# Decoder layer on one core: key rows in two other buffers, seven casts put ahead of copies, early scores half a tile sooner

## The chip, the cores and the metric

The kernel runs on one core of a Trainium2 chip. A core has five engines that run beside each other, each with its own queue of instructions: TensorE (PE, matrix products and transposes through the array; its weight loads are listed apart as PEld), VectorE (DVE), ScalarE (ACT), GpSimd (POOL) and SyncE (SP, which here only issues transfers between the main memory and the core). They wait for one another through semaphores. An engine takes its instructions in the order of its queue, so one that waits holds up all behind it.

The metric is the time of one execution on the device in microseconds (us). The profile is of one execution; its span runs from the first to the last instruction.

## The reference, cut to what matters

One layer of a decoder, for a prompt of 2048 tokens (D_MODEL 1024) and for 8 sequences of 4 sample tokens with 8192 earlier tokens each in a paged cache. All is in float32.

```python
h = rms_norm(x, pre_g)
z = h @ w_in                     # 11 parts of 512 columns
ca, cb, cg, pu, pg, q, k, v, sg, mq, mg = split(z)
mk, mv = split(rms_norm(mem, g) @ w_mem_kv)     # 256 memory tokens
y_c, conv_new = conv_branch(ca, cb, ...)        # depthwise conv of 31 taps, LayerNorm, pointwise
y_p, pool_new = pool_branch(pu, ...)
y_s = sb_fn(q, k, v, sb_bias)                   # stick-breaking attention, 8 heads x 64
y_m = mem_attend(mq, mk, mv)                    # softmax attention, 4 heads x 128
mix = concat([y_c * silu(cg), y_p * silu(pg), y_s * silu(sg), y_m * silu(mg)])
out = rms_norm(mix @ w_out, post_g)
return x + out, conv_new, pool_new, k, v        # then a last rms_norm; k, v, mk, mv are outputs too
```

## The kernel before

**Stages.** First the projection `z = h @ w_in`, which lasts for some 1490 us and has the cache attention of the sample tokens, the convolution and the memory attention woven into it; then the stick-breaking attention of the prompt; then the product with `w_out`. The prompt goes through the projection in two parts of 1024 tokens; part 0 carries the 32 sample tokens too.

**The projection.** `z_groups` (L786) goes over groups of weight columns (128 columns of one kind: q, k, v, ca and so on), and in each over tiles of tokens: three in part 0 (384, 384, 288), two of 512 in part 1. One tile is a product of 24 matmuls (`mm3`, L236): eight slices of the depth, three products each, because a float32 value is split into a high and a low part of a faster type. The generator yields after half of the 24 and after the tile; at every yield the main loop makes one step of all running tasks, and a task puts its own matmuls between two half tiles of the projection. "Half a tile" in the title is one such step.

**Weights.** `load_w` (L222) loads 128 columns (512 KB) through SP into one of two buffers `wr`; `split_w` (L229) casts them on ACT to the high part `whi` (L232) and subtracts on POOL or DVE for the low part `wlo` (L233); both have two buffers. A cast can run once the load is there and the product that used its buffer has ended; the next load can go once the subtract is done. `fill_w` keeps two weights split and two loaded.

**Memory tokens.** Between the tiles of q2, q3 and k0 in part 0, `mem_tokens` (L404) makes eight products of the memory (`mz`, 256 columns) with weights of its own, in one order with the others. `mem_rows` evacuates them (L424) and splits them for the attention (L418, L419).

**Evacuation.** `z_evac` (L674) takes a finished tile from PSUM. For q and k, ACT copies it to `zt` (L683), DVE casts the high part `hl` (L685), POOL subtracts the low part (L686), and SP stores both (L688). For k and v the task `natural` (L364) transposes `zt` on PE (L370), ACT copies the rows to `nat` (L372), and SP stores them to the output (L375).

**Buffers.** `small` is a tag of four buffers of 128 x 512, shared by `zt`, `nat` of k, gate tiles and others. `mkT` and `mvn` are one buffer each of the same size; the memory attention loads keys and values of one head into them (`mem_kv`, L667). A new tile of a tag waits until an old one has been used for the last time; for a tile that is stored, until the store has landed.

**Histories.** `params_and_histories` loads rows of old states (`ht`, L462) and transposes them on PE (`hps`, L478) between tiles of q2.

**Early scores.** When the sample's cache attention has ended, `sb_early` (L1260) loads keys and queries of the first two blocks of the prompt's attention (L1236, L1237), waits some steps, and makes the first two score tiles `Se` (L1253) between the last half tiles of the projection; ACT turns them into gates (L1257, L1258). DVE and POOL then form the weights.

**Order.** Only PE runs in the order in which the program was written (`manual_schedule`). The queues of ACT, DVE, POOL and SP are put in order by a planner, which runs the program on a model clock and takes what is ready. `tc.issue_after(ins)` adds an edge: what the block issues on the engine of `ins` stands behind `ins` in that engine's queue. It is an order, not a wait.

Of the kernel before, what the change touches and what calls it, by code (L numbers as in the profile page):

```python
# [8 lines left out]
F32 = mybir.dt.float32  # L9
# [9 lines left out]
P = 128  # L19
D = 1024  # L20
# [16 lines left out]
SMALL = 4  # L37
# [50 lines left out]
def kernel(  # L88
# [9 lines left out]
    pe, act, dve, pool, sp = nc.tensor, nc.scalar, nc.vector, nc.gpsimd, nc.sync  # L98
# [52 lines left out]
    def tp_tile(name):  # L151
        return tps.tile([P, 512], F32, tag="tp", name=name)

    def z_tile(name):
        return zps.tile([P, 512], F32, tag="z", name=name)
# [12 lines left out]
    table = [act.activation(out=first, in_=eps_t, func=AF.Sqrt)]  # L168
# [53 lines left out]
    def load_w(it):  # L222
# [3 lines left out]
        wq.dma_start(raw_, src[:, o : o + P].rearrange("(d p) n -> p d n", p=P))  # L226
        return raw_

    def split_w(raw, nm):  # L229
        lo = wp.tile([P, ND, P], F32R, tag="wlo", name=f"wlo{nm}", bufs=2)  # L230
        hi = wp.tile([P, ND, P], F32R, tag="whi", name=f"whi{nm}", bufs=2)
        act.copy(hi, raw)  # L232
        (dve if nm in SECOND else pool).tensor_tensor(out=lo, in0=raw, in1=hi.bitcast(F32), op=ALU.subtract)  # L233
        return hi, lo

# [13 lines left out]
    st = zx.enter_context(tc.tile_pool(name="st", bufs=2, side="left"))  # L249
# [5 lines left out]
    def small(name):  # L255
        return st.tile([P, 512], F32, tag="small", name=name, bufs=SMALL)

    def k4(name, shape, dt):
        return st.tile(shape, dt, tag="k4", name=name, bufs=K4)
# [104 lines left out]
    def natural(zt, N, np_, tok, c, out_ap, scratch, srow, nm):  # L364

        yield
        nb = np_ // P
        pt = tp_tile(f"nt{nm}")
        for j in range(nb):
            pe.transpose(pt[:, P * j : P * (j + 1)], zt[:, P * j : P * (j + 1)], ident)  # L370
        nat = small(f"nat{nm}") if scratch is None else k4(f"nat{nm}", [P, D], F32)
        act.copy(nat[:, : np_], pt[:, : np_])  # L372
        nv = nat[:, : np_].rearrange("p (j n) -> p j n", n=P)
        dst = out_ap[tok : tok + np_, P * c : P * (c + 1)].rearrange("(j p) n -> p j n", p=P)
        wq.dma_start(dst, nv)  # L375
        if scratch is not None:
            wq.dma_start(scratch[tok : tok + np_, P * c : P * (c + 1)].rearrange("(j p) n -> p j n", p=P), nv)
        if N > np_:
            pt2 = tp_tile(f"ns{nm}")
            pe.transpose(pt2[:NS, :P], zt[:, np_:N], ident)  # L380
            nat2 = small(f"nas{nm}")
            act.copy(nat2[:NS, :P], pt2[:NS, :P])
            for dst in srow:
                wq.dma_start(dst[:, P * c : P * (c + 1)], nat2[:NS, :P])
# [19 lines left out]
    def mem_tokens(mp, M):  # L404

        for c in range(8):
            ps = z_tile(f"mz{c}")
            for _ in mm3(ps, *wsplit[0, "mem", c], M["hi"], M["lo"], 0, NMEM):
                pass
            del wsplit[0, "mem", c]  # L410
            fill_w()
            tasks.add(mem_rows(mp, ps, c))
            yield
# [230 lines left out]
        for r0, r1, dst in rows:  # L644
            wq.dma_start(dst, o[r0:r1])

    state = {"att": 0, "early": 0}

    def z_open(part, kind, c):

# [23 lines left out]
    def z_evac(part, kind, c, ti, c0, c1, ps, s):  # L674
        a0 = PART * part
        N = c1 - c0
        np_ = min(c1, PART) - c0
        nm = f"{part}{kind}{c}_{ti}"
        tok = a0 + c0
        if kind in ("q", "k"):  # L680
            zt = small(f"zt{nm}")
            with tc.issue_after(table[6].ins) if nm == "0q0_0" else ExitStack():
                act.activation(out=zt[:, :N], in_=ps[:, :N], func=AF.Copy, scale=0.125 if kind == "q" else 1.0)  # L683
            hl = k4(f"hl{nm}", [P, 2, 512], F32R)
            dve.tensor_copy(hl[:, 0, :np_], zt[:, :np_])  # L685
            pool.tensor_tensor(out=hl[:, 1, :np_], in0=zt[:, :np_], in1=hl[:, 0, :np_].bitcast(F32),  # L686
                               op=ALU.subtract)
            wq.dma_start((qd if kind == "q" else kd)[c, :, :, tok : tok + np_], hl[:, :, :np_].bitcast(F32))  # L688
            if N > np_:
                pool.tensor_copy((qsT if kind == "q" else ksT)[:, c, :], zt[:, np_:N])  # L690
            if kind == "k":
                tasks.add(natural(zt, N, np_, tok, c, kp, None, (kso,), nm))
        elif kind == "v":
            zt = small(f"zt{nm}")
            act.copy(zt[:, :N], ps[:, :N])
            tasks.add(natural(zt, N, np_, tok, c, vp, vd, (vso, vsd), nm))
        elif kind in ("cg", "sg", "pg", "mg"):
            sg = small(f"sg{nm}")
            act.activation(out=sg[:, :N], in_=ps[:, :N], func=AF.Sigmoid)
            if kind == "pg":  # L700
                dve.tensor_tensor(out=sg[:, :N], in0=ps[:, :N], in1=sg[:, :N], op=ALU.mult)
                tasks.add(pool_out(c, state["d"], part, c0, c1, ti, sg, s["plw"]))
            elif kind == "mg":
                gt = state["g"][:, c0:c1]
                dve.tensor_tensor(out=gt, in0=ps[:, :N], in1=sg[:, :N], op=ALU.mult)
                if N > np_:
                    pool.tensor_copy(gms[:, c, :], gt[:, np_:N])
            else:
                dve.tensor_tensor(out=sg[:, :N], in0=ps[:, :N], in1=sg[:, :N], op=ALU.mult)
                gdst = gcd if kind == "cg" else gsd  # L710
                wq.dma_start(gdst[c, :, tok : tok + np_], sg[:, :np_])
                if N > np_:
                    if kind == "cg":
                        wq.dma_start(gcd[c, :, SEQ : SEQ + NS], sg[:, np_:N])
                    else:
                        pool.tensor_copy(gss[:, c, :], sg[:, np_:N])
        elif kind == "ca":
            U = s["U"]
            act.copy(U[:, CH + c0 : CH + c0 + np_], ps[:, :np_])
            if N > np_:  # L720
                act.copy(us_s[:, c, :, CH:], ps[:, np_:N].rearrange("p (b t) -> p b t", t=TS))
        elif kind == "cb":
            U = state["U"]
            sg = small(f"sg{nm}")
            act.activation(out=sg[:, :N], in_=ps[:, :N], func=AF.Sigmoid)
            uu = U[:, CH + c0 : CH + c0 + np_]
            pool.tensor_tensor(out=uu, in0=uu, in1=sg[:, :np_], op=ALU.mult)
            if N > np_:
                uv = us_s[:, c, :, CH:]
                pool.tensor_tensor(out=uv, in0=uv, in1=sg[:, np_:N].rearrange("p (b t) -> p b t", t=TS),  # L730
                                   op=ALU.mult)
        elif kind == "pu":
            pf = s["pf"]
            act.copy(pf[:, PH + c0 : PH + c0 + np_], ps[:, :np_])
            if N > np_:
                act.copy(ps_s[:, c, :, PH:], ps[:, np_:N].rearrange("p (b t) -> p b t", t=TS))
        elif kind == "mq":
            hl = k4(f"mh{nm}", [P, 2, 512], F32R)

            act.activation(out=hl[:, 0, :N], in_=ps[:, :N], func=AF.Copy, scale=-(P ** -0.5))  # L740
            dve.scalar_tensor_tensor(out=hl[:, 1, :N], in0=ps[:, :N], scalar=-(P ** -0.5), in1=hl[:, 0, :N].bitcast(F32),
                                     op0=ALU.mult, op1=ALU.subtract)
            if N > np_:
                dve.tensor_copy(mqs[:, c, :], ps[:, np_:N])
            state["att"] += 1
            tasks.add(mem_attend(c, part, c0, np_, hl, state["g"], s["kv"]))
# [22 lines left out]
    raw, wsplit = {}, {}  # L769
# [490 lines left out]
    def sb_early(load, blk, sbr, bps, early):  # L1260

        room = sbr.tile([P, 16, P], F32, tag="V", name="early", bufs=2).rearrange("p (n j b) c -> p n j (b c)", n=4, j=2)
        for n in range(2):
            blk[0, n] = load(0, n)
        for _ in range(4):
            yield
        for hh in range(2):
            S = bps.tile([P, 512], F32, tag="AT", name=f"Se{hh}", bufs=2).rearrange("p (j k) -> p j k", j=2)
            Q, KT, _ = blk[0, 0]
            sb_scores(S, hh, 0, 2 * P, Q[hh], KT[0, hh, 0])  # L1270
            early[hh] = room[:, 2 * hh], room[:, 2 * hh + 1]
            sb_gates(S, hh, 2 * P, *early[hh])
            yield
# [541 lines left out]
    with tc.tile_pool(name="mem", bufs=2, side="right") as mp:  # L1815
# [23 lines left out]
        mem = mem_tokens(mp, M)  # L1839
# [29 lines left out]
    due, blk, early = 0.0, {}, {}  # L1869
# [269 lines left out]
```

## Time and profile before

| | |
|---|---|
| median of 3 runs | 2387.06 us (2386.06 to 2393.02) |
| the profiled execution | 2387.03 us |
| its span | 2385.3 us |
| mean granted clock of TensorE | 0.987 |
| waits of PE on ACT, POOL or a transfer, at places that the change touches | the rows mz, hps, nt0k, nt1k, z1k and S of the table of waits |
| mean load of the transfer engines | 234 GB/s |

How to read it. A row of a timeline is: start (us from the span's start), length, engine, line of the kernel, operation, what is written and what is read, shape, how many were merged (x3), and in brackets how long the engine had been idle and what it waited for. Tiles of one kind share a name: `zt0k` is a tile of keys of part 0, `nt1k` the transposes of keys in part 1, `whi0mem` the high part of a memory weight. A row of the table of waits is: total us, times, longest. A row of the table by stretches gives busy time and number of instructions of PE, PEld, DVE, ACT and POOL, then the clock that TensorE was granted (1.00 is full), the share of the transfer engines, and GB/s.

### The profile page before, as it was taken

To read this page: it belongs to the slowest core of one execution; us is meant where nothing else is said; L and a number is where in the kernel's file an instruction comes from. 1 tells how busy PE (TensorE), PEld (TensorE's weight loads), DVE (VectorE), ACT (ScalarE), POOL (GpSimd) and SP (SyncE) were. 2 spreads that over 40 slices of the span, in tenths; PEclk is the share of its full clock that TensorE was granted. 3 is DMA by queue.
4 is the path that set the end of the run, shared out by engine and by line. 5 is a ranking of instruction groups with operands and counts; after the bars stand their busy time and mean duration, and the time that the engine had idled before them with its cause. 6 is when DMAs were issued, how large, how long until landed. Compare 5 with 4: busy or idle time off the path is not lost. (4 is left out here: it accounts for less than half of the span.)

```text
span 2385.3 us, 42238 instructions
## 1 busy us (share of the span) xinstructions
PE 2283.3 (96%) x16024; PEld 1774.9 (74%) x16024; DVE 1717.9 (72%) x2428; ACT 1120.3 (47%) x1947; POOL 1282.7 (54%) x1322
## 2 busy tenths in 40 slices
PE   7999999999999999999999999799999999989996
PEld 7898888888888677777777777455555557878875
DVE  5342796969657564577787868878888966777897
ACT  5322243242442222234242424788899875444554
POOL 3454545555565555545546462699877763531231
PEclk9999999999999999999999999899999999999999
DMA  6678977878778899987877875667443206866774
GB/s 212 196 257 290 349 270 259 286 249 291 246 262 316 296 327 331 327 283 260 305 263 262 269 268 150 165 201 215 123 107 79 78 19 218 289 196 207 238 236 162
DMA packets 336869, 557.94 MB, mean 234 GB/s; under 512 B 27986, under 2 KB 212434, under 8 KB 320267
## 3 DMA queue, kind: packets, MB, share of 16 engines
q1 hardware_dynamic: 281290, 286.53, 38.7%
q0 software_dynamic: 55376, 268.72, 31.8%
q8 instruction: 126, 2.06, 0.3%
q14 instruction: 77, 0.62, 0.1%
HBM read 465.09 MB, written 90.68 MB: 233 GB/s over the span
## 5 line engine op out<-in xcount | busy, mean ns | idle before, releaser
L957 DVE STREAM_TRANSPOSE T<-kt 128x1024 f32<-128x1024 f32 x256 | 308.7, 1226 | 190.0 <-PE sSA L970 179.0
L924 POOL DMA_INDIRECT vt<-in_cache_v_dram,idv x256 | 252.8, 987 | 261.6 <-PE sO L1009 200.6
L610 DVE SCALAR_TENSOR_TENSOR cacc<-U,par,cacc 128x512 f32<-128x512 f32 x480 | 359.9, 750 | 11.0
L1335 POOL TENSOR_TENSOR be<-be,E 128x512 f32<-128x512 f32 (+3 forms) x316 | 300.7, 963 | 70.0 <-DVE E L1326 22.5
L1326 DVE TENSOR_TENSOR_SCAN E<-gam,cr,ZM 128x513 f32<-128x513 f32 x192 | 233.3, 1264 | 23.3 <-ACT gam L1257 13.9
L924 POOL DMA_INDIRECT kt<-in_cache_k_dram,idk x128 | 128.5, 1004 | 195.0 <-DVE T L957 152.1
L1346 PEld LDWEIGHTS AT<-ident,be 128*128 128x128 f32 x1082 | 118.1, 143 | 137.0 <-ACT at L1352 40.9
L1959 PE MATMUL acc<-wohi,mh 128*128 128x512 f32 (+1 forms) x480 | 193.3, 403 | 1.5 <-ACT mh L1704 0.8
L1257 ACT ACTIVATE gam<-S,nbias_bc 128x1024 f32<-128x1024 f32 (+1 forms) x158 | 170.2, 1077 | 47.3 <-ACT be L1258 15.4
L1959 PE MATMUL acc<-wolo,mh 128*128 128x512 f32 (+1 forms) x480 | 189.0, 394 | 0.0
L1346 PE MATMUL AT<-ident,be 128*128 128x128 f32 x1082 | 161.4, 286 | 20.9 <-DVE at L1350 9.1
L1253 PE MATMUL S<-kT,Q 128*128 128x512 f32 (+1 forms) x632 | 176.5, 403 | 4.8 <-ACT be L1258 4.8
L1959 PE MATMUL acc<-wohi,ml 128*128 128x512 f32 x448 | 176.9, 395 | 4.1 <-DVE ml L1715 4.1
L1258 ACT ACTIVATE be<-S,bias_bc 128x1024 f32<-128x1024 f32 (+1 forms) x158 | 169.1, 1070 | 0.0
L1362 PE MATMUL av<-at,V 128*64 128x512 f32 (+3 forms) x640 | 153.1, 558 | 3.9 <-DVE sbo L1367 3.9
L970 PE MATMUL sSA<-T,W 128*32 128x128 f32 x4096 | 140.5, 277 | 2.3 <-DVE T L957 1.4
L970 PEld LDWEIGHTS sSA<-T,W 128*32 128x32 f32 x4096 | 105.6, 110 | 37.4 <-issue 30.8
L1009 PE MATMUL sO<-vt,saT 128*32 128x512 f32 x1024 | 122.3, 592 | 0.0
L1253 PEld LDWEIGHTS S<-kT,Q 128*128 128x128 f32 x632 | 106.7, 196 | 18.2 <-ACT be L1258 5.4
L1323 DVE TENSOR_TENSOR_SCAN E<-gam,ZM 128x384 f32<-128x384 f32 (+1 forms) x124 | 94.6, 811 | 33.1 <-ACT gam L1257 25.7
L1352 ACT COPY at<-AT 128x512 f32<-128x512 f32 x192 | 108.9, 650 | 20.1 <-PE AT L1346 19.9
L1715 DVE TENSOR_TENSOR ml<-mr,mh 128x512 fp32r<-128x512 f32 x108 | 87.2, 812 | 30.7 <-ACT mh L1704 30.6
(577 smaller groups left out, 6039.9 us busy)
## 6 DMA issues: line engine op xcount, KB each, us to landing
Q<-qd SPq DMA_DIRECT2D x64, 256.0 KB
mr<-mixd SPq DMA_DIRECT2D x32, 512.0 KB
mr<-mixd SPq DMA_DIRECT2D x48, 256.0 KB
xtp<-in_x_prompt_dram SPq DMA_DIRECT2D x16, 512.0 KB
kT<-kd SPq DMA_DIRECT2D x64, 128.0 KB
ws<-in_w_out_dram SPq DMA_DIRECT2D x16, 512.0 KB
wsd<-ws SPq DMA_DIRECT2D x16, 512.0 KB
msd<-mr SPq DMA_DIRECT2D x32, 256.0 KB
```

Source lines behind the costliest of these rows:

```text
L610: dve.scalar_tensor_tensor(out=ps, in0=U[:, a + k : a + k + H], scalar=wd[:, k : k + 1], in1=ps, op0=ALU.mult, op1=ALU.add)
L924: pool.indirect_dma_start(out=dst, out_offset=None, in_=rows, in_offset=bass.IndirectOffsetOnAxis(ap=idx, axis=0))
L957: S["turn"] = dve.transpose(T[:, 2 * hh : 2 * hh + 2].rearrange("p s j t -> p (s j t)"), kt[:, 2 * hh : 2 * hh + 2].rearrange("p s j d -> ...
L970: pe.matmul(sSs[n][32 * g : 32 * g + 32, P * ml : P * (ml + 1)], lhsT=W[:, jj, :], rhs=T[:, :, jj, :], start=i == 0, stop=i == 3, tile_pos ...
L1253: pe.matmul(S[:, j, :w], lhsT=Q[:, x, P * (q2 + j) : P * (q2 + j + 1)], rhs=kt[:, :w], start=x == 0, stop=x == 1)
L1257: act.activation(out=ga, in_=S[:, :, :w], func=AF.Sigmoid, bias=nbias_bc[:, h : h + 1], scale=-1.0)
L1258: act.activation(out=be, in_=S[:, :, :w], func=AF.Sigmoid, bias=bias_bc[:, h : h + 1])
L1326: dve.tensor_tensor_scan(out=E[:, j][:, ::-1], data0=g_[:, j][:, ::-1], data1=ZM[:, 0:1].to_broadcast([P, 513]), initial=carry[hh, q2][:, ...
L1335: pool.tensor_tensor(out=be[:, j, :m], in0=be[:, j, :m], in1=E[:, j, 513 - w : 513 - w + m], op=ALU.mult)
L1346: pe.transpose(ap_[:, P * qt : P * (qt + 1)], A[hp, qb, kc, hh, qt][:, P * r : P * (r + 1)], ident)
L1362: pe.matmul(av[64 * hh : 64 * hh + 64, c], lhsT=V[:, 4 * kc + r, 64 * hh : 64 * hh + 64], rhs=ats.pop((hp, qb, kc, r, hh))[:, c], start=dg ...
L1959: pe.matmul(o[:rows], lhsT=m[a][:, k, :rows], rhs=W[prod, 4 * h + k][w], start=not cont and h == k == n == 0, stop=h == 1 and k == 3 and n ...
```

## The change

Three things. A row tile of keys takes the buffers `mkT`, `mvn` and `small` in turn, by a counter that runs over all 20 of them, where all came from `small`. While the memory products run (from product 0 up to and not including product 7), the copy `zt` of a q or k tile stands behind the newest weight cast in ACT's queue. And `sb_early` waits three steps instead of four before its scores.

```diff
+    casts = []
+
     def split_w(raw, nm):
         lo = wp.tile([P, ND, P], F32R, tag="wlo", name=f"wlo{nm}", bufs=2)
         hi = wp.tile([P, ND, P], F32R, tag="whi", name=f"whi{nm}", bufs=2)
-        act.copy(hi, raw)
+        casts.append(act.copy(hi, raw))
...
         for j in range(nb):
             pe.transpose(pt[:, P * j : P * (j + 1)], zt[:, P * j : P * (j + 1)], ident)
-        nat = small(f"nat{nm}") if scratch is None else k4(f"nat{nm}", [P, D], F32)
+        if scratch is None:
+            tag = ("mkT", "mvn", "small")[state["nat"] % 3]
+            state["nat"] += 1
+            nat = st.tile([P, 512], F32, tag=tag, name=f"nat{nm}", bufs=SMALL if tag == "small" else 1)
+        else:
+            nat = k4(f"nat{nm}", [P, D], F32)
...
         for c in range(8):
+            state["mem"] = c < 7
             ps = z_tile(f"mz{c}")
...
-    state = {"att": 0, "early": 0}
+    state = {"att": 0, "early": 0, "mem": False, "nat": 0}
...
             zt = small(f"zt{nm}")
-            with tc.issue_after(table[6].ins) if nm == "0q0_0" else ExitStack():
+            before = table[6] if nm == "0q0_0" else casts[-1] if state["mem"] else None
+            with tc.issue_after(before.ins) if before is not None else ExitStack():
                 act.activation(out=zt[:, :N], in_=ps[:, :N], func=AF.Copy, scale=0.125 if kind == "q" else 1.0)
...
         for n in range(2):
             blk[0, n] = load(0, n)
-        for _ in range(4):
+        for _ in range(3):
             yield
```

## The prediction

> **What bounds the kernel now.** I read the page first (busy times, slices), then the table of waits for TensorE alone, then the timelines of all engines around each of its waits in the projection. The page:
>
> ```profile
> span 2385.3 us, 42238 instructions
> ...
> PE 2283.3 (96%) x16024; PEld 1774.9 (74%) x16024; DVE 1717.9 (72%) x2428; ACT 1120.3 (47%) x1947; POOL 1282.7 (54%) x1322
> ```
>
> PE works 96% of the span, its order is written by hand, and no other engine is above 74%. So time is won only where PE stands still, 102 us in all, or runs slowly. The table of PE's waits over the whole span (total us, how often, longest) has these rows for what the change touches:
>
> ```profile
> PE S L1253 <- ACT be L1258: 4.8, 2, 3.0
> ...
> PE nt0k L370 <- ACT zt0k L683: 3.5, 2, 2.1
> PE nt1k L370 <- ACT zt1k L683: 2.5, 1, 2.5
> PE z1k L242 <- ACT xhi L218: 2.5, 1, 2.5
> PE mz L242 <- POOL wlo0mem L233: 2.4, 1, 2.4
> ...
> PE hps L478 <- DMA ht<-in_state_conv_dram: 1.3, 1, 1.3
> PE mz L242 <- ACT whi0mem L232: 1.2, 1, 1.2
> ```
>
> A wait also costs what comes after it. In the table by stretches (length; PE, PEld, DVE, ACT, POOL busy; granted clock; DMA) these follow a wait directly; the second one follows the shorter of the two nt0k waits (3.5 less 2.1 is 1.4):
>
> ```profile
> 66.00:70.00 4.00, 3.72 (x19) 3.72 (x19) 0.00 (x0) 0.00 (x0) 0.23 (x1) 0.58 0.55 163
> 122.00:126.00 4.00, 4.00 (x24) 3.99 (x25) 2.19 (x1) 0.52 (x2) 2.97 (x3) 1.00 0.82 251
> 152.00:156.00 4.00, 4.00 (x20) 4.00 (x19) 0.09 (x1) 1.44 (x3) 1.01 (x1) 0.58 1.05 424
> 794.00:798.00 4.00, 4.00 (x11) 2.93 (x11) 3.79 (x6) 0.03 (x1) 0.00 (x0) 0.61 0.30 114
> 832.00:836.00 4.00, 4.00 (x42) 2.96 (x42) 1.36 (x3) 0.59 (x1) 3.62 (x2) 0.67 0.81 298
> ```
>
> After the waits of 2.1 us and more the granted clock falls to about 0.6 for four microseconds, a loss of 4 x 0.42 = 1.7 us (66, 152), 1.6 (794) and 1.3 (832); after the short wait it stays at 1.00.
>
> **Part 1: the cast ahead of the copy.** The edge ties seven copies (q2_1 to k0_1), but in the timeline six of them already stand behind the cast in question. Only q2_1's moves:
>
> ```profile
> 61.95 0.49 ACT L683 ACTIVATE zt0q<-z0q 128x384 f32<-128x384 f32 x1 [4.23 <-PE z0q L242]
> 62.34 1.04 ACT L232 CAST whi0mem<-wr0mem 128x1024 fp32r<-128x1024 f32 x1
> ```
> ```profile
> 58.59 1.00 POOL L686 TENSOR_TENSOR hl0q<-zt0q,hl0q 128x384 fp32r<-128x384 f32 x1 [4.13 <-ACT mhlk L418]
> ...
> 63.89 2.34 POOL L233 TENSOR_TENSOR wlo0mem<-wr0mem,whi0mem 128x1024 fp32r<-128x1024 f32 x1
> ```
> ```profile
> 51.47 0.56 SPq L226 DMA_DIRECT2D wr0mem<-in_w_mem_kv_dram  x1
> ...
> 66.26 0.37 SPq L226 DMA_DIRECT2D wr0q<-in_w_in_dram  x1
> ...
> 67.30 0.44 SPq L462 DMA_DIRECT2D ht<-in_state_conv_dram  x1
> ```
> ```profile
> 53.88 0.28 PE L242 MATMUL mz<-mhi,whi0mem 128*128 128x256 f32 x1
> ...
> 56.59 0.28 PE L242 MATMUL mz<-mhi,wlo0mem 128*128 128x256 f32 x1
> ...
> 61.69 0.57 PE L478 MATMUL hps<-ident,ht 120*128 120x120 f32 x4
> ...
> 71.97 0.60 PE L478 MATMUL hps<-ident,ht 120*128 120x120 f32 x4 [1.31 <-DMA ht<-in_state_conv_dram]
> ```
>
> ACT stood idle 4.23 us in front of the copy, and the weight behind it had been asked for at 51.47, ten microseconds earlier. The cast's buffer is free when memory product 0 ends, 56.59 + 0.28 = 56.87. So it goes there: cast to about 58, POOL's subtract (2.34, with the 1.00 of hl0q before or after it) to 60.3 to 61.9. PE wants it at 61.69 + 0.57 = 62.3: both mz waits go, 3.6 us, and with them the slow stretch. Product 1 then needs what product 0 took (53.88 to 56.87, 3.0 us) and ends at 65.3. Now something else is late: the next transposes need the histories' rows, whose load stands on SP behind wr0q's, and that waits for the same subtract (63.89 + 2.34 = 66.23). With qd's store, which waits for hl0q, also in that queue, I put wr0q's load at 62.0 instead of 66.26, the histories' 1.04 later, their arrival again 71.97 - 67.30 = 4.67 after the issue: 67.7 instead of 71.97. Gain 4.3. Bounds: 3.4, if hl0q and the subtract are queued the worse way round; 6.7, if the planner puts the histories' load first (71.97 to 65.3). The new wait, 67.7 - 65.3 = 2.4 us, may bring a slow stretch of 1.7; I take off half, 0.9. [...]
>
> **Part 2: key rows in idle buffers.** 20 row tiles (12 in part 0, 8 in part 1) leave the four small buffers in two of three cases. Nothing is added: same copies, same stores. What waited for the buffers:
>
> ```profile
> 151.15 0.49 ACT L683 ACTIVATE zt0k<-z0k 128x384 f32<-128x384 f32 x1 [4.72 <-DMA out_dram<-nat0k]
> ...
> 792.47 0.59 ACT L372 COPY nat1k<-nt1k 128x512 f32<-128x512 f32 x1 [2.06 <-DMA out_dram<-nat1k]
> ...
> 831.10 0.60 ACT L683 ACTIVATE zt1k<-z1k 128x512 f32<-128x512 f32 x1 [3.79 <-DMA out_dram<-nat1k]
> ```
>
> All three waits are for a store that still reads a small buffer. With one row tile in three there, the buffer that each copy gets is four allocations old and holds no open store. At 151 PE gains 2.1 + 1.7 = 3.8; at 831, 2.5 + 1.3 = 3.8: in both the copy waited longer (4.72, 3.79) than PE did (2.1, 2.5), so without the store it is there when PE asks. The 1.4 us wait near 121 stays: its copy is behind a cast, not a store. At 792 it is the row copy itself, with the x casts queued behind it on ACT; without its wait they run 2.06 us sooner, but their DVE subtracts do not:
>
> ```profile
> 789.74 2.33 DVE L610 SCALAR_TENSOR_TENSOR cacc<-U,par,cacc 128x512 f32<-128x512 f32 x3
> 793.58 1.29 DVE L219 TENSOR_TENSOR xlo<-xpsp,xhi 128x512 fp32r<-128x512 f32 x2 [1.51 <-ACT xhi L218]
> ```
>
> DVE is free at 792.07, so PE's second product comes 793.58 - 792.07 = 1.5 us sooner, and the 1.6 of the slow stretch goes or not: 1.5 to 3.1, I take 2.2 (with xlo moved as well, the full 2.5 + 1.6 = 4.1). Queues: the two single buffers are reloaded for the memory attention, and these loads now go behind the last key stores on SP instead of early:
>
> ```profile
> L501 PE MATMUL ms<-mkT,mh0mq x96: 276/279/388, 335.8 to 699.6; 128*128 128x256 f32 x96
> ...
> L669 SPq DMA_DIRECT2D mkT<-mkd x8: 319/385/745, 75.7 to 1364.8; - x8
> ```
>
> The first load moves from 75.7 to about 165; its first reader is at 335.8. The old owner is done at 699.6, 80 us before part 1's first row tile. I price the move at nothing; SP's idle time covers it (rival 2 has the case without).
>
> **Part 3: early scores.** Eight matmuls change places with half a tile; PE's sum is the same.
>
> ```profile
> 1490.42 0.59 ACT L616 COPY acc<-cacc 128x512 f32<-128x512 f32 x1 [6.64 <-DVE cacc L610]
> 1490.90 0.70 ACT L1257 ACTIVATE early<-Se,nbias_bc 128x512 f32<-128x512 f32 x1
> ...
> 1493.67 1.15 ACT L1257 ACTIVATE gam<-S,nbias_bc 128x1024 f32<-128x1024 f32 x1
> ```
> ```profile
> 1478.93 0.60 SPq L1237 DMA_DIRECT2D Q<-qd  x1
> ```
> ```profile
> 1487.17 0.64 PE L1253 MATMUL Se<-kT,Q 128*128 128x256 f32 x4
> ```
>
> The scores were there from 1487.8, but ACT stood 6.64 us at the copy of the convolution's sum. The copy, four gates of the scores and one activation more then run to 1493.67. If the planner, seeing the scores sooner, puts the four gates (1490.42 to 1493.67 is 3.25, two of its six run 0.48, so four take 2.3) ahead of that copy, the attention's first gates and PE's S wait (4.8) come 2.3 sooner; if not, nothing. I take 1.1. On the other side: the last load that both scores need is issued at 1478.93, and Se would start at about 1484.4, 5.5 us later, above the 4.67 of part 1; were the loads as late as today's start, PE would lose 2.8.
>
> **Sum:** 4.3 - 0.9 + 3.8 + 3.8 + 2.2 + 1.1 = 14.3 us. The profiled execution took 2387.03 us (span 2385.3 and 1.7 around it), the median of the runs is 2387.06, so both give 2372.7. After 850 us nothing in the PE table is bound to a fixed time (most waits lie in the attention and the output, on ACT, DVE and POOL), so the gain should reach the end.
>
> **Rivals.** (1) Refilled stalls, time within 0.3%: PE finds the next-late thing at each place. Histories' rows as late as now, DVE's subtract at 792 as late as now, no early gates: only 3.8 + 3.8 stay, less 1.7 for one more slow stretch, 5.9: 2381.1. For it: in part 1 of the sum two other things really are late by 2.4 and 1.5. Against: at 151 and 831 I see none.
> (2) SP held by the moved loads: a load of mkT or mvn behind a key store waits for that store to land. Place: SP from 850. Price: in the crowded stretch a row store issued at 784.52 freed its buffer at 792.47, 8 us, so the weight load due at 853.81 would go some 5 us late:
>
> ```profile
> 784.52 0.66 SPq L375 DMA_DIRECT2D out_dram<-nat1k  x1
> ...
> 853.81 0.38 SPq L226 DMA_DIRECT2D wr1v<-in_w_in_dram  x1
> ```
> ```profile
> 876.27 1.05 ACT L232 CAST whi1v<-wr1v 128x1024 fp32r<-128x1024 f32 x1 [3.21 <-PE z1v L242]
> ```
>
> Its cast is 22 us after the issue (876.27), so it decides only when the hold passes about 16 us; then each further us is lost, and the gain of 14 is gone at a hold of 30: about 2387. [...]
> (3) Slower: the planner orders ACT, DVE, POOL and SP by a clock of its own, and both new rules shift that clock for everything behind them. Place: the sample's 64 blocks, PE scores, ACT gates, DVE scan, PE transposes, where PE hardly waits now. A gate put behind a row copy (0.59) in each block would cost up to 64 x 0.59 = 38 us; it decides from 14.3 / 64 = 0.22 us a block; at 0.4 the time is 2387 - 14.3 + 25.6 = 2398. For it: PE's order is fixed and can't give way. Against: the edges touch 57 to some 110 us and the buffers two short stretches.
>
> **Chances.** Forecast 0.78, refilled 0.11, SP held 0.04 (half of it slower), planner's order 0.07. 0.3% of 2387 is 7.2 us, about what a measurement here can tell from no change. Faster 0.78, same 0.13, slower 0.09. Range: the best of all terms is 6.7 + 3.8 + 3.8 + 4.1 + 2.3 = 20.7, 2366, with 1 us spare; upwards it takes in rival 1 and a little loss to the new order, 2383.
>
> **What the profile after would show.** Right: whi0mem near 57 to 58 and ahead of zt0q, the two mz rows gone from PE's waits, hps waiting 2 to 3 us instead; no wait of ACT for nat0k or nat1k stores, rows nt1k gone and nt0k down to 1.4; z1k waiting for xlo, about 1.5; the granted clock 1.00 around 152 and 832; gates of Se ahead of acc. The forecast fails if PE's table has new rows in the sample's blocks, or a weight row for v in part 1.

## The result and the profile after

The changed kernel takes 2381.61 us (median of 18 runs, 2373.86 to 2392.21), the kernel before, measured beside it, 2388.41 us (18 runs, 2383.04 to 2396.03). The ratio is 0.9972, with a 95% interval of 0.9962 to 0.9982: 6.8 us faster, between 4.3 and 9.1. The forecast was 14.3 us, 2372.7. The sign was right; less than half of the gain came.

The profiled execution of the changed kernel took 2378.62 us. The head of its page:

```profile
span 2376.9 us, 42227 instructions
...
PE 2279.8 (96%) x16024; PEld 1772.0 (75%) x16024; DVE 1720.7 (72%) x2428; ACT 1119.1 (47%) x1947; POOL 1277.5 (54%) x1322
```

TensorE (PE) now idles 2376.9 - 2279.8 = 97.1 us, where it was 102.0. Its table of waits (total us, how often, longest) has, for what the change touches:

```profile
PE S L1262 <- ACT be L1267: 4.8, 2, 3.0
PE hps L486 <- DMA ht<-in_state_conv_dram: 2.7, 1, 2.7
...
PE nt0k L372 <- ACT zt0k L692: 1.3, 1, 1.3
...
PE smt L1175 <- DMA mkb<-in_cache_mem_k_dram: 1.0, 1, 1.0
PE nt0v L372 <- ACT zt0v L704: 1.0, 1, 1.0
...
PE z1k L244 <- ACT xhi L218: 0.3, 1, 0.3
```

The rows of mz and nt1k are gone, nt0k is down to the 1.3 behind a cast, z1k to 0.3, and the histories' wait has grown to 2.7. At each place aimed at, the profile shows what was meant. S is as before. Two rows are new, nt0v and smt, 1.0 each.

Stretches of the changed kernel at those places (PE, PEld, DVE, ACT, POOL busy; granted clock; DMA share; GB/s):

```profile
66.00:70.00 4.00, 1.99 (x16) 2.00 (x16) 2.80 (x6) 0.97 (x3) 2.35 (x1) 1.00 0.79 287
138.00:142.00 4.00, 4.00 (x20) 4.00 (x20) 2.06 (x14) 0.00 (x0) 3.33 (x4) 0.61 1.08 364
150.00:154.00 4.00, 4.00 (x26) 3.96 (x25) 2.22 (x1) 1.14 (x5) 3.28 (x3) 1.00 0.67 229
786.00:790.00 4.00, 3.48 (x18) 2.54 (x17) 3.77 (x7) 1.54 (x4) 0.00 (x0) 1.00 1.01 331
828.00:832.00 4.00, 4.00 (x57) 2.27 (x55) 1.57 (x2) 1.43 (x3) 0.43 (x1) 1.00 1.12 362
```

The clock is full where it had dropped to about 0.6. But it drops at a place where it had not, 138 to 142 us, although PE is busy for all of the four microseconds around it.

Laid side by side by their matmuls, the two traces are 13 us apart at 2037 us and 8.4 at the end: the changed kernel seems to lose 4.5 us in the output stage. The queues' orders are the same in both from 1545 us on. That made the first question: does the output stage hand the gain back, do new waits eat it, or is one of the two profiles an odd draw?

### The profile page after: what moved, and what is told of

It reads as the page before. It is cut to its first block, busy times and chain, and to the rows that moved or that the text cites. A ratio compares the mean times of both kernels' runs of the same rounds, so it can differ in the third digit from the quotient of the medians.

```text
span 2376.9 us, 42227 instructions
## 1 busy us (share of the span) xinstructions
PE 2279.8 (96%) x16024; PEld 1772.0 (75%) x16024; DVE 1720.7 (72%) x2428; ACT 1119.1 (47%) x1947; POOL 1277.5 (54%) x1322
```

## The experiments

**How a profile is taken apart.** The span is cut at the same matmuls in every kernel. In each stretch I take PE's idle time, and half of the busy time that lies at half clock. These two are what the change can move; what is left of the span is 2260 to 2264 us in all kernels. Theory A: the stalls were real and their removal reaches the end, but the forecast priced them from one execution, and they differ from one to the next. Theory B: the output stage hands gain back. Theory C: the new waits nt0v and smt, and the drop at 138 us, belong to the change. Theory D: part 3 costs something, by moving gates and loads to a worse place.

**One part at a time.** First the cast alone:

```diff
-        act.copy(hi, raw)
+        casts.append(act.copy(hi, raw))
...
+            state["mem"] = c < 7
...
-            with tc.issue_after(table[6].ins) if nm == "0q0_0" else ExitStack():
+            before = table[6] if nm == "0q0_0" else casts[-1] if state["mem"] else None
+            with tc.issue_after(before.ins) if before is not None else ExitStack():
```

> Kernel: the kernel before with part 1 alone (the cast of a memory weight ahead of the product tiles' copies). Theory A (the idle time that the change removes is real and reaches the end; the slow-clock stretches behind the stalls were counted as certain, but occur in only about half of the executions): the two mz waits (3.6 us) are gone, the histories' wait grows from 1.3 to about 2.7, so 2.2 us less idle time and about half of a 1.7 us stretch: about 3 us faster in the median (1.5 to 4), and the end of TensorE's work is as much earlier as the stretch behind 70 us, give or take slow stretches that come and go in the output stage in either direction. Theory B (the output stage hands back 4 to 5 us whenever the work ahead of it comes sooner): 3 to 4 us earlier at 1550 us, no earlier at the end, ratio 1.000. Theory C (part 1 itself costs something later, the slow stretch at 138 us being its doing): earlier by 4 at 70 us, by 2.7 from 142 us on, and a slow stretch right behind the histories' 32-column products in this profile too.

Then the key rows alone:

```diff
-        nat = small(f"nat{nm}") if scratch is None else k4(f"nat{nm}", [P, D], F32)
+        if scratch is None:
+            tag = ("mkT", "mvn", "small")[state["nat"] % 3]
+            state["nat"] += 1
+            nat = st.tile([P, 512], F32, tag=tag, name=f"nat{nm}", bufs=SMALL if tag == "small" else 1)
+        else:
+            nat = k4(f"nat{nm}", [P, D], F32)
```

> Kernel: the kernel before with part 2 alone (key rows in turn in the two idle buffers and the small ones). Theory A: idle time removed at 147, 789 and 821 us is 2.2 + 2.0 + 2.5 = 6.7 us, new waits nt0v and smt (1.0 each) take 2.0 of it, and of the three slow stretches of 1.6 about half count in the median: 4.7 + 2.4, so about 6 to 7 us faster (4.5 to 8). Theory B: about 9 us earlier at 1550 us, 4 to 5 of it lost again in the output stage, 4 to 5 us faster, with the loss at the same rows as in the changed kernel (2050 to 2080 and 2240 us). Theory C (the new waits nt0v behind 210 us and smt behind 960 us belong to part 2): both rows are in this profile at about 1.0 each, and not in that of part 1 alone.

The early scores alone:

```diff
-        for _ in range(4):
+        for _ in range(3):
             yield
         for hh in range(2):
```

> Kernel: the kernel before with part 3 alone (the early scores half a tile sooner). Theory A: nothing ahead of 1470 us changes; the wait S stays at 4.8 us, since the copy of the convolution's sum stays ahead of the gates; gain 0 to 1.5 us, not to be told from none. Theory B: as A, and the output stage stays as it was, since its work starts at most 1.5 us sooner. Theory D (the planner moves loads and gates at this place to the bad): slower by 1 to 3 us, with a longer wait of the first scores or of the first scan.

And the changed kernel with that last edit undone, so parts 1 and 2 together:

> Kernel: the changed kernel with the early scores back in their old place (parts 1 and 2 without part 3). Theory A: within 1.5 us of the changed kernel, so 5 to 8 us faster than before. Theory B: the same total, and the output stage loses 4 to 5 us against the kernel before, as it does in the changed kernel. Theory D (part 3 is what loses): 9 us or more faster than before, the output stage as before or the first scan sooner.

Measured beside 35 runs of the kernel before (median 2389.93), with 12 runs each:

```
                       median us   ratio    95% interval
part 1 alone           2385.93     0.9985   0.9975 to 0.9994
part 2 alone           2384.72     0.9984   0.9972 to 0.9996
part 3 alone           2393.18     1.0013   1.0000 to 1.0025
parts 1 and 2          2383.51     0.9978   0.9964 to 0.9991
```

Part 1 is worth 3.6 us (1.4 to 6.0), as forecast (3.4). Part 2 is worth 3.8 (1.0 to 6.7), not 9.8, and less than the 6 to 7 expected of it alone. Part 3 gains nothing that can be told: alone its interval begins at no change and lies on the slower side (3.1 us slower, 0 to 6.0, where Theory A expected a gain of 0 to 1.5), and without it the changed kernel has 0.9978, with it 0.9972, each inside the other's interval. Theory D is neither shown nor excluded by this: the longer wait of the first scores that it expected isn't there, S is 4.8 in part 3 alone as before (a small wait of ACT that part 3 brings is told further below). From 1960 us to the end, idle time and the loss to half clock together are:

```
kernel before, first profile   40.4
changed kernel                 44.8
part 1 alone                   44.9
part 2 alone                   43.1
part 3 alone                   44.9
parts 1 and 2                  44.0
```

Part 3 alone changes nothing ahead of 1470 us and brings the output stage no earlier (its trace is 3.5 us behind there), and it has the same 44.9. So Theory B falls: the odd one is the profile of the kernel before. Theory C falls as well for nt0v: the row of 1.0 stands in all four, part 3 alone among them, and below in the unchanged kernel. The row smt stands in none of the four, nor in any other profile shown below.

**The stalls differ between executions.** Part 1 alone leaves the small buffers as they were. Its table of waits has no row for nt1k (2.5 us in the first profile), but more of the other two:

```profile
PE nt0k L372 <- ACT zt0k L687: 5.8, 3, 2.4
...
PE z1k L244 <- ACT xhi L218: 2.9, 1, 2.9
```

So the unchanged kernel was profiled again, three times, and the changed one twice.

> The kernel before, unchanged, a second profiled execution. Theory A (the first profile of the kernel before was a lucky draw in the stretches that no edit touches, and the four kernels with parts of the change show the usual values): from 1960 us to the end the idle time and the loss to slow-clock stretches are together 43 to 45 us, not the 40.4 of the first profile, and from 200 to 760 us TensorE idles 5.5 to 7 us, not 4.3; the span is 2386 to 2391. The stalls that the change aims at vary too: idle and slow loss 7 to 8 us from 40 to 100 us, 4 to 7 from 100 to 200, 3.5 to 9 from 760 to 860. Theory B (the output stage loses 4 to 5 us because of the change): 40 to 41 us again from 1960 us on.

> The changed kernel, unchanged, a second profiled execution. Theory A: idle and slow loss 3.5 to 5 us from 40 to 100 us and 1.0 from 760 to 860 us as before, since those stalls are gone for good; from 100 to 200 us anything from 3.5 to 9, since the wait for a key store at 150 us comes back in some executions; 43 to 45 from 1960 us on; median 6 to 8 us below the kernel before. Theory B: the same span, and from 100 to 200 us the 3.9 of the first profile again.

> The kernel before, unchanged, a third profiled execution, for how often the stalls that part 2 removes occur at all. Theory A (their size is set by when a store lands, and that differs from one execution to the next): the sum of ACT's waits for key rows' stores that reach TensorE (nt0k beyond its 1.3, nt1k, z1k beyond 0.3) lies anywhere from 2 to 7 us; the first profile had 6.8, the second 2.2. From 1960 us on idle and slow loss are 43 to 46 us. Rival (the second profile was the odd one): 6 to 7 us again, and idle and slow loss of 8 to 9 us from 760 to 860 us.

> The kernel before, unchanged, a fourth profiled execution: as for the one before it. Theory A: idle and slow loss from 760 to 860 us anywhere from 2 to 9 us, mean over the executions without part 2 about 6, not the 8.7 that the prediction was made from.

> The changed kernel, unchanged, a third profiled execution. Theory A: 1.0 us of idle time from 760 to 860 us and 3.5 to 3.8 from 40 to 100 us, as in both profiles so far; from 100 to 200 us 2.0 to 2.2, unless the wait for a row store at 150 us comes back (once in five executions with part 2 so far).

In the second profile of the kernel before, PE's waits have these rows:

```profile
PE nt0k L370 <- ACT zt0k L683: 2.3, 2, 1.3
PE z1k L242 <- ACT xhi L218: 1.5, 1, 1.5
...
PE nt0v L370 <- ACT zt0v L695: 1.0, 1, 1.0
```

and in the third:

```profile
PE nt0k L370 <- ACT zt0k L683: 3.9, 2, 2.6
PE z1k L242 <- ACT xhi L218: 2.9, 1, 2.9
...
PE nt0v L370 <- ACT zt0v L695: 1.0, 1, 1.0
...
PE nt1k L370 <- ACT zt1k L683: 0.9, 1, 0.9
```

The same program waits 0, 0.9 or 2.5 us for nt1k. For the first and the second profile of the kernel before, the stretch from 760 to 860 us reads so (columns as above):

```profile
760.00:860.00 100.00, 94.52 (x743) 72.88 (x741) 57.79 (x74) 29.59 (x54) 52.33 (x49) 0.97 0.89 303
```
```profile
760.00:860.00 100.00, 97.82 (x811) 75.70 (x810) 62.72 (x80) 32.93 (x60) 56.84 (x51) 1.00 0.94 327
```

PE stands still for 5.5 us in the one and 2.2 in the other, and the clock is 0.97 in the one and full in the other. All kernels without the edits of the next paragraphs, idle time plus loss to half clock, cut at the same matmuls:

```
                       40-100  100-200  760-860  1460-1540  1960-end
before, 1st profile    7.4     6.0      8.7      15.8       40.4
before, 2nd            7.5     3.1      2.2      14.0       46.5
before, 3rd            7.8     6.4      7.4      14.1       45.1
before, 4th            7.4     5.7      6.4      13.4       43.2
part 3 alone           7.6     4.3      9.2      13.9       44.9
part 1 alone           3.6     6.8      3.6      14.1       44.9
part 2 alone           7.7     3.8      1.0      13.4       43.1
parts 1 and 2          5.0     8.8      1.0      13.8       44.0
changed, 1st           3.6     3.9      1.0      13.7       44.8
changed, 2nd           5.5     2.0      1.0      14.0       45.5
changed, 3rd           5.5     2.2      1.0      13.3       45.8
```

From 760 to 860 us the five executions with part 2 all have 1.0; the six without it run from 2.2 to 9.2. That stall is gone for good, but it was not always there. The means with and without the part in question differ by 2.9 us (40 to 100, part 1), 1.2 (100 to 200, part 2), 5.3 (760 to 860, part 2) and 0.4 (1460 to 1540, part 3): 9.8 in all. The second comparison of the changed kernel gave 2383.14 us (7 runs) against 2389.65, ratio 0.9967 (0.9953 to 0.9980), 7.9 us. The spread was wider than expected: the second profile of the kernel before has 3.1 and 2.2 us where 4 to 7 and 3.5 to 9 stood, and 46.5 where 43 to 45 stood. The second of the changed kernel misses its ranges too, with 5.5 where 3.5 to 5 stood, 2.0 where 3.5 to 9 stood and 45.5 where 43 to 45 stood. The third and the fourth of the kernel before lie inside what Theory A expected, and so does the third of the changed kernel; but in the third of the kernel before the waits for stores make 6.1 us, which its rival, 6 to 7, allowed as well.

**The wait that came back.** With parts 1 and 2, one execution lost 8.8 us between 100 and 200 us. Its ACT and its SP queue:

```profile
154.92 0.41 ACT L692 ACTIVATE zt0k<-z0k 128x288 f32<-128x288 f32 x1 [5.21 <-DMA out_dram<-nat0k]
```
```profile
140.00 0.56 SPq L382 DMA_DIRECT2D out_dram<-nat0k  x1
```

The same two in the first profile of the changed kernel:

```profile
149.99 0.40 ACT L692 ACTIVATE zt0k<-z0k 128x288 f32<-128x288 f32 x1
```
```profile
137.91 0.56 SPq L382 DMA_DIRECT2D out_dram<-nat0k  x1
```

In part 0 a group has three tiles, and the rotation puts the third one's row tile, with the sample rows (nas) behind it, in small buffers. In a ring of four, the next group's third product tile then gets the buffer of that row tile, whose store was issued 12 to 15 us before. In one execution it had landed by 149.99, in the other not until 154.9. Theory: give the sample rows the free columns of the row tile, so that every small buffer returns to its own user after a whole group.

```diff
-            nat2 = small(f"nas{nm}")
+            nat2 = small(f"nas{nm}") if scratch is not None else nat[:, 384:512]
```

> The changed kernel, with the sample tokens' key rows (32 x 128) written into free columns of the row tile that was just filled instead of a small buffer of their own, so that in part 0 each of the four small buffers comes back to its own user after a whole group of three tiles, and no product tile follows a stored row tile of the group before. Theory A (the wait at 150 us came back because a product tile takes the small buffer of a row store issued some 10 to 15 us earlier, in a stretch where the transfers are full): idle from 100 to 200 us 2.1 to 2.3 (the wait of 1.3 behind the weight's cast alone), no wait of the product tiles' copies for a store there, and 1.5 to 3 us faster in the median than the changed kernel. Rival (the transfers, not the buffer, hold the copy): the wait shows again under another name, no faster.

To this the histories' rows, asked for earlier:

```diff
-        prow = mp.tile([P, 512], F32, tag="ht", name="prow")
+        prow = mp.tile([P, 512], F32, tag="ht", name="prow", bufs=3)
...
-                hts.append(mp.tile([P, 512], F32, tag="ht", name=f"ht{hist}_{b0}"))
+                hts.append(mp.tile([P, 512], F32, tag="ht", name=f"ht{hist}_{b0}", bufs=3))
...
         load()
+        load()
         for _ in range(4):
             yield
```

> The kernel of the run before it, with a third buffer for the histories' rows and their second load asked for at once, not after the parameters' transposes. Theory A: the histories' wait of 2.7 us near 66 us is gone or down to what was there for other rows, 40 to 100 us idles 1 us instead of 3.6, so 2 to 3 us faster than the run before it, and the slow stretch behind it cannot occur. Rival: the load stands on SP in the same place, behind the weight's load, and nothing changes.

And both of these without part 3, so with four half tiles ahead of the early scores again:

> The two edits of the earlier runs (key rows of the sample tokens in the row tile's free columns; a third buffer for the histories) on the changed kernel without part 3. Theory A: the wait for the first gates, which had grown from 4.8 to 6.6 and 8.1 us in those two, is a matter of the planner's order near 1490 us; with the early scores in their old place it is 4.4 to 4.8 again, and the kernel takes 2379 to 2382 us, about as the best so far. Rival (the third buffer or the free columns cause that wait): 6 us or more again.

The sample rows in the row tile gave 2384.51 us (12 runs, 0.9982, 0.9971 to 0.9994): not faster than the changed kernel beside it, which misses the expectation. ACT's product tiles wait for no store there in any of the three, but in two of them the row copy itself does, 4.50 us in the one with the sample rows alone and 5.10 in the last one. So the rival was half right. PE waits 0.7 for it in the last one and nothing in the other:

```profile
154.91 0.37 ACT L379 COPY nat0k<-nt0k 128x256 f32<-128x256 f32 x1 [4.50 <-DMA out_dram<-nat0k]
```
```profile
155.65 0.37 ACT L379 COPY nat0k<-nt0k 128x256 f32<-128x256 f32 x1 [5.10 <-DMA out_dram<-nat0k]
```

With the histories it is 2381.58 (6 runs, 0.9962, 0.9949 to 0.9976); from 40 to 100 us PE idles 2.9 instead of 3.5, not 1: the rows that were late are in time, and the next ones are late by 2.3, since their load is still behind a weight's on SP, and the half-clock stretch that was expected not to occur is there, 1.7. So the 2.9 us by which this kernel's median lies below the run before it are in the expected range, 2 to 3, but the stretch shows only 0.6 less idle time: most of that number is not this edit's, as far as one profile tells. Without part 3 it is 2379.17 (6 runs, 0.9958, 0.9942 to 0.9974), the lowest of all, but its interval overlaps that of the changed kernel.

The wait S is 6.6 and 8.1 us in the two of these that have part 3, and 4.8 in the one that has not, as Theory A expected. ACT in the first profile of the changed kernel, and then in the one with the histories:

```profile
1479.46 0.59 ACT L624 COPY acc<-cacc 128x512 f32<-128x512 f32 x1 [6.64 <-DVE cacc L618]
1479.95 0.70 ACT L1266 ACTIVATE early<-Se,nbias_bc 128x512 f32<-128x512 f32 x1
...
1482.24 0.62 ACT L708 ACTIVATE sg1sg<-z1sg 128x512 f32<-128x512 f32 x1
1482.71 1.15 ACT L1266 ACTIVATE gam<-S,nbias_bc 128x1024 f32<-128x1024 f32 x1
...
1488.41 0.69 ACT L1267 ACTIVATE be<-S,bias_bc 128x512 f32<-128x512 f32 x1 [0.42 <-DMA gsd<-sg1sg]
```
```profile
1492.18 1.11 ACT L1268 ACTIVATE be<-S,bias_bc 128x1024 f32<-128x1024 f32 x1 [3.35 <-DMA gsd<-sg1sg]
```

The copy of the convolution's sum stayed ahead of the early gates, and instead the planner moved the gate sg1sg, which stood behind two of them, behind all four. A later gate then waits for its store, 0.42 us in the one and 3.35 in the other (2.14 in the one with the sample rows alone, 0.82 in part 3 alone). All six executions with part 3 have such a wait, 0.21 us the shortest, and none of the eight without it.

## Why the prediction was wrong

**The step that failed** is the price of part 2 at 151 us, 2.1 + 1.7 = 3.8. The runs show 1.2 there, the difference of the means: 1.5 of idle time in place of the 2.1, and a loss of 0.3 to half clock in place of a gain of 1.7. Five executions stand against six here and one of the five, the 8.8, weighs much: without it the 1.2 would be 2.4. So the term was priced too high, by how much is uncertain by 1 us and more. Two steps led to it. The sentence that "the buffer that each copy gets is four allocations old and holds no open store" is half false: four allocations old, yes, but in part 0 the third product tile's buffer held a row store, and in one of the five executions it was still open 14.9 us after its issue. In part 1, too, the first profile of the changed kernel has ACT waiting for a key row's store, 3.78 us at 845 us, where the prediction expected no such wait; PE pays nothing for it. And a half-clock stretch was counted as won, where the executions with part 2 have between 100 and 200 us 1.7, 0, 0, 1.7 and 2.1 us of it and those without 0 to 1.7.

**Beside it, a sum made from one draw.** The three waits on stores were read as fixed sizes. From 760 to 860 us the first profile lost 8.7 us and the mean of the six executions without part 2 is 6.2. Over the three stretches of parts 1 and 2 it lost 22.1 us where the means are 7.6 + 5.4 + 6.2 = 19.2. That did not show in its time, since elsewhere it was lucky: 40.4 from 1960 us on, where the others in the table have 43.1 to 46.5. A time near the median says nothing about whether each of its stalls is.

**Part 1** came as worked out. In the changed kernel ACT and POOL run:

```profile
57.91 1.05 ACT L234 CAST whi0mem<-wr0mem 128x1024 fp32r<-128x1024 f32 x1
...
58.87 1.00 POOL L695 TENSOR_TENSOR hl0q<-zt0q,hl0q 128x384 fp32r<-128x384 f32 x1 [4.13 <-ACT mhlk L426]
59.82 2.39 POOL L235 TENSOR_TENSOR wlo0mem<-wr0mem,whi0mem 128x1024 fp32r<-128x1024 f32 x1
```

Both mz waits are gone and the histories wait 2.7, forecast 2.4. Half a chance for a slow stretch behind them was right too: 3 of the 5 executions with part 1 have it, 1.5 to 1.7 us. 3.4 was forecast, 2.9 is the difference of the means, 3.6 the time of part 1 alone.

**At 792 and 831 us** 6.0 was forecast and 5.3 came on average. At 792 the mechanism was better than forecast: DVE's subtract moved with the casts, which had been the upper bound, as the planner put it ahead of the convolution's steps:

```profile
786.48 1.06 ACT L218 CAST xhi<-xpsp 128x512 fp32r<-128x512 f32 x2
787.09 1.29 DVE L219 TENSOR_TENSOR xlo<-xpsp,xhi 128x512 fp32r<-128x512 f32 x2
```

At 831 the wait was removed, but its mean over the executions that could have it is 1.2 us, not 2.5.

**Part 3** was forecast at 1.1, the middle of 0 and 2.3. It is at the lower end: the gates stayed behind the copy, and what moved was sg1sg. The means differ by 0.4, and the time of part 3 alone shows no gain.

**The rivals.** The number of the first, 2381.1, is close to the result, but not by its reasons: histories and DVE came as well as forecast or better, and the term that it kept, 151 us, is the one that failed. The moved loads of mkT and mvn stand at 159 to 164 and 837 to 847 us and hold nothing: no row of PE's table waits for a weight of v. The sample's blocks are not slower: from 860 to 1460 us PE idles 2.1 to 2.9 us in the changed kernel, and 1.9 to 2.1 in the kernel before.

**What stays open.** The differences in the stretches make 9.8 us, 4.5 less than the forecast: 2.6 at 151 us, 0.7 at 792 and 831, 0.7 in part 3, 0.5 in part 1. But the two comparisons make 6.8 and 7.9, the mean spans of the profiles 8.2 (2388.5 of four, 2380.3 of three). The rest is not placed: in the stretches that no edit touches, single executions differ by 6 us, more than what is missing.

**The drop at 138 us** comes with 32 products of 32 columns (`qps`). In the changed kernel they begin at 135.78, and from 138.88 to 142.29 the granted clock is 0.50, although PE is busy for all of the 3.41 us ahead. In the kernel before the same 32 take 3.65 us from 139.69 on at a clock of 1.00, so the products are not the change's own. The drop was seen in four of the eight executions with part 2, counting the three kernels with further edits, and in none of the six without it. The changed kernel itself has it in its first profile and not in its second, where the clock is 1.00 from 100 to 200 us. So it is no fixed price of part 2; whether part 2 makes it likelier, 14 executions do not tell, and for this drop Theory C stays open. What brings it on was not shown.

## What to carry to other kernels

A wait that ended with a DMA's landing was a draw here, not a constant (nt1k cost 0, 0.9 or 2.5 us in one and the same program; from 828 to 832 us, where the 2.5 lie, the DMA share was 1.07): price it from several profiled executions, above all where the transfers are full, and keep zero as its lower end. When buffers are handed out in turn, write down for each user whose buffer it gets and when that store was issued; "four allocations old" is a count, and what matters is the age in microseconds (here a store was still open 14.9 us after its issue). When a profile after a change seems to lose time in a stage that the change can't reach, profile the unchanged kernel again before looking for a cause there.

## What the runs showed of the hardware

In the traces of the kernel before and of the changed kernel, every stretch below full clock has a granted clock of 0.50. Away from the end of the span each lasts 3.41 or 6.83 us. The four that the prediction counted begin at 66.65, 151.99, 793.69 and 831.24 us and last 3.41 us each; in the 3.41 us ahead of them PE was busy for 0.25, 0.37, 0.27 and 0.42 of the time.

The length of a stall alone does not tell whether such a stretch comes. The wait of 2.7 us for the histories, which ends at 68.01 us in the changed kernel, left the clock at 1.00 from 64 to 72 us; the wait of 2.1 us that ends at 151.70 us in the kernel before was followed by 0.50 from 151.99 to 155.40. Over all 14 profiled executions of this case, of 27 stalls of 2.0 to 2.9 us with less than 0.3 us of other idle time within 3.4 us on either side, 20 brought a half-clock stretch, of 44 of 1.5 to 2.0 us 7. At 138.88 us in the changed kernel it came behind 3.41 us in which the profile has PE busy all the time.

The row store of 128 KB (128 x 256 f32) near 140 us was still open 14.9 us after its issue in one execution and had landed within 12.1 us in another, in a stretch where the DMA share is 1.00 to 1.08 (138 to 150 us, in both).
